# Inputs ahead of most first weights, squares on VectorE, statistics and roundings at given places

## The chip, the core and the metric

The program runs on one core of one Trainium2 chip. The metric is the device time of one execution in microseconds. TensorE (PE in the profile) multiplies, VectorE (DVE) and ScalarE (ACT) round, add and activate, GpSimd (POOL) adds and issues accumulating DMAs, SyncE (SP) issues most loads.

## What is computed

An encoder layer on two sequences of 256 tokens with 1024 features each: a feed-forward of half weight, a mixer (two recurrent branches with gates), a second feed-forward, and a last normalisation. The change touches the first feed-forward and the end of the second.

```python
def rmsnorm(x, g):
    xf = x.astype(jnp.float32)
    y = xf * lax.rsqrt(jnp.mean(xf * xf, axis=-1, keepdims=True) + EPS)
    return (y * g.astype(jnp.float32)).astype(x.dtype)

def swiglu(h, w_in, w_out):
    a, g = jnp.split(h @ w_in, [D_FF], axis=-1)
    return (jax.nn.silu(a) * g) @ w_out

def encoder_layer(x, ...):
    x = x + 0.5 * swiglu(rmsnorm(x, g_ffn1), w_ffn1_in, w_ffn1_out)
    h = rmsnorm(x, g_mix)
    ...
    x = x + merged.astype(x.dtype) @ w_out
    x = x + 0.5 * swiglu(rmsnorm(x, g_ffn2), w_ffn2_in, w_ffn2_out)
    return x

y = rmsnorm(encoder_layer(x, ...), g_final)
```

## The kernel before

**Layout.** The input stands transposed: eight tiles x0 to x7 of 128 features by 512 tokens (both sequences side by side). Every product is made of three passes, since each operand is split into a rounded high half (names with h: `xh`, `wah`, `wbh`) and a remainder, the low half (`xl`, `wal`, `wbl`). A high half is a copy on ScalarE. A low half is either a subtraction on VectorE (`split2`, L240) or, with `split_dma` (L244 to L246), a negated copy on ScalarE to which a DMA issued by POOL then adds the source once more.

**First feed-forward, first products.** `first_tiles` multiplies the eight inputs with the first six column tiles of the weights, for k = 0 to 7: three passes of six matmuls each, 18 for each k, all at L277. SP loads x_k and then the weights of k, in the order of k (L121, L123). Each weight tile is rounded when it has landed; from k = 6 on (`dma_from` 3) the low half comes by `split_dma`. `split_x` makes the two halves of x_k, scaled by the gain, and `add_sq` squares x_k on ScalarE and adds it on GpSimd to the sum `sq`.

**Statistic.** `rms_stat` runs with high priority: four small products with a column of ones sum `sq` over the features (L163, tile `ps_f1p`), ScalarE takes the root (L151, for which a table is loaded), VectorE refines the reciprocal in small steps (L152 to L156) and writes a diagonal (L177), and TensorE spreads it over all partitions (L182). ScalarE copies the result to `r` (L194). The normalisation itself is applied behind the products, in `gated`.

**Input sums and plain pairs.** `x_sums` builds, in four steps k = 0 to 3, sums and differences of quarter inputs (`xu`, `xv`, `xt`, `xw`, each scaled by `r`), which the later column tiles need; each is split (`xch`, `xcl`). Meanwhile two pairs of column tiles run as plain products (`f1p`, then `f1p2`, in `plain`, L218 to L220), each with two weight tiles of 1024 columns that `w_plain` loads and rounds by `split_dma`. Behind them `pair` runs the other column tiles (L344).

**The order.** A scheduler places instructions on each engine by priorities; `issue_after(i)` keeps what is written in it behind instruction i. At the end, in `last2`, the order of TensorE, VectorE and ScalarE is written by hand: the last residual add and its square for each half (256 tokens, one sequence), the statistic of each half, and four tiles y of each half, each sent by a DMA of its own, in turn from ScalarE's and SP's queue (L1000).

## Time and profile before

| | us |
|---|---|
| median of 3 runs | 1192.49 (1192.47 to 1193.64) |
| profiled execution | 1191.2 |
| its span | 1189.4 |
| TensorE busy | 1172.2 (99%) |
| VectorE, ScalarE, GpSimd busy | 733.0, 608.7, 115.8 |

A time in a row of the profile counts from the span's start. A row of the timeline is one instruction, or several equal ones in a row: start, duration, engine, line and operation, output and inputs with shapes, count, and in brackets how long the engine had been idle and what released it. The start of the next row can lie a little before the end of one, since instructions on an engine overlap. Buffer numbers are left out of names.

### The profile page before, as it was taken

The page shows a single profiled execution, that of the slowest core. Times are in us where ns is not written, and L with a number is a line of the kernel's source. Part 1 is how long each engine was busy: PE and PEld are TensorE (multiplying, and loading weights), DVE is VectorE, ACT ScalarE, POOL GpSimd, SP SyncE. Part 2 cuts the span into 40 slices and gives each one's busy share as a digit, 9 for nine tenths or more (in the row PEclk, how much of TensorE's full clock was granted, in tenths as well). Part 3 has the DMA queues.
Part 4 walks back from the last instruction along what each step waited for, and adds up shares of the span by engine and source line. Part 5 has one row for each costly group of instructions (what it writes and reads, how often), then busy time and mean ns, then how long its engine had stood idle before and what let it go on. Part 6 is the DMA issues. An engine that isn't in the chain of part 4 may idle for free.

```text
span 1189.4 us, 16897 instructions
## 1 busy us (share of the span) xinstructions
PE 1172.2 (99%) x6654; PEld 1016.4 (85%) x6654; DVE 733.0 (62%) x1124; ACT 608.7 (51%) x991; POOL 115.8 (10%) x143
## 2 busy tenths in 40 slices
PE   8999999999999999999999999999999999999996
PEld 6898899899987888888888888888789899989985
DVE  7974576567546888657573453363685467566643
ACT  7663365256536666575762232255664256336542
POOL 5100000000022002020000000013200000000011
PEclk9999999999999999999999999999999999999998
DMA  8763555356414213232253233141854356445512
GB/s 253 167 161 105 139 137 140 117 134 166 122 58 128 89 55 115 72 107 71 80 186 115 89 98 115 55 123 27 204 136 139 114 130 154 132 120 147 152 47 71
DMA packets 58160, 141.88 MB, mean 119 GB/s; under 512 B 5408, under 2 KB 19904, under 8 KB 58080
## 3 DMA queue, kind: packets, MB, share of 16 engines
q1 hardware_dynamic: 47664, 110.44, 29.1%
q0 software_dynamic: 8208, 27.94, 13.5%
q10 hardware_dynamic: 2208, 2.41, 0.6%
q8 instruction: 52, 0.85, 0.3%
q14 instruction: 28, 0.23, 0.1%
HBM read 135.51 MB, written 2.11 MB: 116 GB/s over the span
## 4 chain that ended last, share of the span: by engine, by line
PE 90%; issue 5%; DMA 2%; DVE 1%; POOL 1%; ACT 1%; SPq 1%; DVEq 0%; ACTq 0%; POOLq 0%
PE psy_f L344 16%; PE psq_f L344 8%; PE psz_f L344 4%; PE ps_f1o L219 3%; PE ps_f1o L220 3%; PE ps_f1o L218 3%; PE ps_f2o L219 3%; PE ps_f2o L218 3%; PE ps_f2o L220 3%; PE pt_ga L577 3%; PE pt_ga L575 3%; PE pt_ga L576 2%; PE pt_gb L577 2%; PE pt_gb L575 2%; PE pt_gb L576 2%
## 5 line engine op out<-in xcount | busy, mean ns | idle before, releaser
L344 PE MATMUL psy_f<-xch_f,wal_f2s 128*128 128x256 f32 x204 | 57.5, 282 | 0.2 <-DMA wal_f2s<-in_w_f 0.2
L344 PE MATMUL psy_f<-xch_f,wal_f1s 128*128 128x256 f32 x204 | 57.4, 281 | 0.2 <-DMA wal_f1s<-in_w_f 0.2
L344 PE MATMUL psy_f<-xch_f,wah_f2s 128*128 128x256 f32 x204 | 57.5, 282 | 0.1
L344 PE MATMUL psy_f<-xch_f,wah_f1s 128*128 128x256 f32 x204 | 57.4, 281 | 0.0
L344 PE MATMUL psy_f<-xcl_f,wah_f2s 128*128 128x256 f32 x204 | 57.4, 281 | 0.0
L344 PE MATMUL psy_f<-xcl_f,wah_f1s 128*128 128x256 f32 x204 | 57.3, 281 | 0.0
L577 PE MATMUL pt_ga<-whi_ga,xl_m 128*128 128x512 f32 x128 | 50.7, 396 | 0.0
L575 PE MATMUL pt_ga<-whi_ga,xh_m 128*128 128x512 f32 x128 | 50.6, 396 | 0.0
L577 PE MATMUL pt_gb<-whi_gb,xl_m 128*128 128x512 f32 x128 | 50.5, 396 | 0.0
L576 PE MATMUL pt_ga<-wlo_ga,xh_m 128*128 128x512 f32 x128 | 50.4, 394 | 0.0
L575 PE MATMUL pt_gb<-whi_gb,xh_m 128*128 128x512 f32 x128 | 50.4, 394 | 0.0
L576 PE MATMUL pt_gb<-wlo_gb,xh_m 128*128 128x512 f32 x128 | 50.4, 394 | 0.0
L94 DVE TENSOR_TENSOR wlo_ga<-raw_ga,whi_ga 128x1024 fp32r<-128x1024 f32 x16 | 19.6, 1225 | 46.0 <-ACT whi_ga L93 46.0
L427 DVE SCALAR_TENSOR_TENSOR x<-ps_f2o,x 128x512 f32<-128x512 f32 x23 | 15.9, 690 | 41.6 <-PE ps_f2o L220 41.6
L93 ACT CAST whi_gb<-raw_gb 128x1024 fp32r<-128x1024 f32 x16 | 16.8, 1048 | 45.7 <-PE pt_ga L577 28.8
L94 DVE TENSOR_TENSOR wlo_gb<-raw_gb,whi_gb 128x1024 fp32r<-128x1024 f32 x16 | 19.6, 1224 | 32.7 <-ACT whi_gb L93 32.5
L344 PEld LDWEIGHTS psy_f<-xch_f,wah_f2s 128*128 128x128 f32 x204 | 38.5, 189 | 0.4 <-ACT f2u L404 0.3
L344 PEld LDWEIGHTS psy_f<-xch_f,wal_f2s 128*128 128x128 f32 x204 | 38.6, 189 | 0.4 <-DMA wal_f2s<-in_w_f 0.4
L344 PEld LDWEIGHTS psy_f<-xch_f,wal_f1s 128*128 128x128 f32 x204 | 38.5, 189 | 0.5 <-DMA wal_f1s<-in_w_f 0.5
L427 DVE SCALAR_TENSOR_TENSOR x<-ps_f1o,x 128x512 f32<-128x512 f32 x24 | 16.6, 690 | 36.1 <-PE ps_f1o L220 36.1
L344 PEld LDWEIGHTS psy_f<-xch_f,wah_f1s 128*128 128x128 f32 x204 | 38.5, 189 | 0.3
L344 PEld LDWEIGHTS psy_f<-xcl_f,wah_f1s 128*128 128x128 f32 x204 | 38.4, 188 | 0.1
(1163 smaller groups left out, 4049.4 us busy)
## 6 DMA issues: line engine op xcount, KB each, us to landing
raw_f1s<-in_w_f SPq DMA_DIRECT2D x17, 512.0 KB, 3.7
wal_f1s<-in_w_f POOLq DMA_DIRECT2D x17, 512.0 KB, 5.5
raw_f2s<-in_w_f SPq DMA_DIRECT2D x17, 512.0 KB, 3.6
wal_f2s<-in_w_f POOLq DMA_DIRECT2D x17, 512.0 KB, 5.6
raw_ga<-in_w_tm SPq DMA_DIRECT2D x16, 512.0 KB, 3.6
raw_gb<-in_w_tm SPq DMA_DIRECT2D x16, 512.0 KB, 3.5
sum_f1s<-in_w_f SPq DMA_DIRECT2D x17, 256.0 KB, 3.2
raw_f1s<-in_w_f SPq DMA_DIRECT2D x17, 256.0 KB, 3.9
```

Of the source, the lines that this page charges most:

```text
L93: nc.scalar.copy(hi[:, :width], raw[:, :width])
L94: nc.vector.tensor_tensor(out=lo[:, :width], in0=raw[:, :width], in1=hi.bitcast(F32)[:, :width], op=ALU.subtract)
L218: nc.tensor.matmul(ps, lhsT=wh, rhs=xh, start=start, stop=False)
L219: nc.tensor.matmul(ps, lhsT=wh, rhs=xl, start=False, stop=False)
L220: nc.tensor.matmul(ps, lhsT=wl, rhs=xh, start=False, stop=stop)
L344: nc.tensor.matmul(ps, lhsT=l[:, f], rhs=m, start=start and k == n == 0, stop=stop and k == 3 and n == 2, skip_group_check=True)
L427: nc.vector.scalar_tensor_tensor(out=x[i], in0=ps, scalar=0.5, in1=x[i], op0=ALU.mult, op1=ALU.add)
L575: nc.tensor.matmul(pss[t], lhsT=xh, rhs=hi[:, ws], start=k == 0, stop=False)
L576: nc.tensor.matmul(pss[t], lhsT=xh, rhs=lo[:, ws], start=False, stop=False)
L577: nc.tensor.matmul(pss[t], lhsT=xl, rhs=hi[:, ws], start=False, stop=k == KD - 1)
```

## The change

The change does seven things.

1. SP's loads: x0, the weights of k = 0, x1, those of k = 1, then x2, x3, x4, the weights of k = 2, x5, x6, x7 and the weights of k = 3 to 7.
2. The first activation of the program, a dummy, is Sqrt instead of a copy; the table that it loads is the one that the statistic needs.
3. In the first feed-forward the squares are no longer made in `split_x`: at k = 0 that of x0, at k = 1 those of x1 to x4, at k = 2 those of x5 to x7 (`squares`), and they are added by VectorE instead of GpSimd.
4. `rms_stat` takes two places (`places`): the sums stand behind the last matmul of pass 1 at k = 2, the broadcast behind that of pass 2 at k = 3.
5. `dma_from` is 4, so the low halves of k = 6 and 7 are subtractions on VectorE.
6. The roundings of the plain pairs stand behind steps of the input sums (`rounds`): the second tile of the first pair and the first tile of the second pair behind step k = 1, the second tile of the second pair behind step k = 2. The first tile of the first pair has no such bound.
7. In `last2` the diagonal of half 0 is written ahead of the residual add of half 1, its broadcast stands ahead of the sums of half 1, and two of the four y of half 0 come ahead of the reciprocal of half 1.

```diff
+    def load_first(k): ...
+    def load_x(k):
+        nc.sync.dma_start(x[k], xT[k * P:(k + 1) * P, :])
+    for k in range(2):
+        load_x(k)
+        load_first(k)
         if k == 0:
             nc.scalar.dma_start(pt, par)
+    for k in range(2, 5):
+        load_x(k)
+    load_first(2)
+    for k in range(5, KD):
+        load_x(k)
+    for k in range(3, KD):
+        load_first(k)
-    nc.scalar.activation(act0, ones[:, 0:1], AF.Copy, scale=2.0)
+    nc.scalar.activation(act0, ones[:, 0:1], AF.Sqrt)
...
+    def at(i):
+        return tc.issue_after(i) if i is not None else ExitStack()
...
-    def rms_stat(sq, name, banks=(None, None)):
+    def rms_stat(sq, name, banks=(None, None), behind=(None, None)):
         with tc.high_priority():
-            rc = rms_cols([sq], range(4), name, banks[0])
-            ps = spread(rc, name, banks[1])
+            with at(behind[0]):
+                st = rms_sum([sq], range(4), name, banks[0])
+            rc = small(f"rc_{name}", 4)
+            rsqrt(rc, st, 1.0 / D, name)
+            dg = diag(rc, name)
+            with at(behind[1]):
+                ps = broadcast(dg, name, banks[1])
...
-            nc.gpsimd.tensor_tensor(out=sq, in0=sq, in1=t, op=ALU.add)
+            (nc.vector if name == "a" else nc.gpsimd).tensor_tensor(out=sq, in0=sq, in1=t, op=ALU.add)
...
                 xs.append(xs_of(k))
+                for n in squares.get(k, ()):
+                    add_sq(n, sq, "a")
...
+                    marks[k, n] = nc.tensor.matmul(pss[m], lhsT=w[:, f[m]], rhs=xp, start=k == n == 0,
+                                                   stop=k == KD - 1 and n == 2).ins
...
                 x_last[:] = [split2(*hl, src).ins]
+                marks["x", k] = rounded[0]
...
-            split_dma(hi, lo, raw, w_a[2 * j + n])
+            with at(behind[n - first]):
+                split_dma(hi, lo, raw, w_a[2 * j + n])
...
-        w_p = w_plain(w_a, NP, f"{name}p")
+        w_p = w_plain(w_a, NP, f"{name}p", (None, None) if rounds is None else (None,))
         for _ in range(4):
             next(steps)
+        if rounds is not None:
+            w_p += w_plain(w_a, NP, f"{name}p", (marks["x", rounds[0]],), 1)
         gated(top, pss[2 * top], pss[2 * top + 1])
-        w_p2 = w_plain(w_a, NP + 1, f"{name}p2")
+        w_p2 = w_plain(w_a, NP + 1, f"{name}p2", (None, None) if rounds is None else [marks["x", n] for n in rounds])
...
-    ffn(w_f1, w_o1, lambda k: split_x(k, C_G1, sq1, "a"), raw1, 3, C_G1, sq1, "f1", done1)
+    ffn(w_f1, w_o1, lambda k: split_x(k, C_G1, None, "a"), raw1, 4, C_G1, sq1, "f1", done1,
+        squares={0: (0,), 1: range(1, 5), 2: range(5, KD)}, places=((2, 1), (3, 2)), rounds=(1, 2))
...
+            dg = [diag(rc[0], "f0")]
             final(1)
-            dg = [diag(rc[0], "f0")]
+            rf = [broadcast(dg[0], "f0")]
             st.append(rms_sum([sq_of("f"), sql], (2, 3), "f1"))
-            rf = [broadcast(dg[0], "f0")]
+            scaled(0, rf[0], range(0, 2))
             rsqrt(rc[1], st[1], 1.0 / D, "f1")
             dg.append(diag(rc[1], "f1"))
             rf.append(broadcast(dg[1], "f1"))
-            for half in range(2):
-                scaled(half, rf[half])
+            scaled(0, rf[0], range(2, KD // 2))
+            scaled(1, rf[1], range(KD // 2))
```

TensorE in the first products, before: the digit after `xh_a`, `xl_a` is k, `wah_f1i1` and `wal_f1i1` are the halves of the weights of k = 2 and 3, `dg_f1` is the diagonal. This is the place of the broadcast.

```order
L277 MATMUL ps_f1i4_147<-xh_a3_238,wal_f1i1_208 128x512
L277 MATMUL ps_f1i5_148<-xh_a3_238,wal_f1i1_208 128x512
L182 MATMUL ps_f1p1_378<-dg_f1_392,ones_75 128x512
L277 MATMUL ps_f1i0_143<-xl_a3_239,wah_f1i1_207 128x512
L277 MATMUL ps_f1i1_144<-xl_a3_239,wah_f1i1_207 128x512
```

The same place of TensorE now:

```order
L295 MATMUL ps_f1i4_147<-xl_a3_254,wah_f1i1_216 128x512
L295 MATMUL ps_f1i5_148<-xl_a3_254,wah_f1i1_216 128x512
L192 MATMUL ps_f1p1_376<-dg_f1_390,ones_75 128x512
L295 MATMUL ps_f1i0_143<-xh_a4_279,wah_f1i2_275 128x512
L295 MATMUL ps_f1i1_144<-xh_a4_279,wah_f1i2_275 128x512
```

The broadcast moved from ahead of the last pass of k = 3 to behind it; the four sums (L163) moved from the middle of the first pass of k = 3 to behind the second pass of k = 2.

ScalarE among the input sums, before: `xch_f1` with two digits is the high half of a sum of the step that the first of the two digits names, `f1p1` is the second tile of the first plain pair, `f1p20` the first of the second.

```order
L239 CAST xch_f10_424<-xu_f10_414 128x256
L244 CAST wbh_f1p20_497<-sum_f1p20_495 128x1024
L239 CAST xch_f100_428<-xv_f10_415 128x512
L239 CAST xch_f10_424<-xu_f11_440 128x256
L245 ACTIVATE wbl_f1p20_498<-sum_f1p20_495 128x1024
L239 CAST xch_f101_432<-xt_f10_416 128x512
L239 CAST xch_f102_436<-xw_f10_417 128x512
L239 CAST xch_f110_452<-xv_f11_441 128x512
L245 ACTIVATE wal_f1p1_410<-raw_f1p1_407 128x1024
L239 CAST xch_f111_456<-xt_f11_442 128x512
L244 CAST wah_f1p1_409<-raw_f1p1_407 128x1024
L239 CAST xch_f112_460<-xw_f11_443 128x512
```

The same place of ScalarE now:

```order
L254 CAST xch_f10_415<-xu_f10_405 128x256
L254 CAST xch_f100_419<-xv_f10_406 128x512
L254 CAST xch_f101_423<-xt_f10_407 128x512
L254 CAST xch_f102_427<-xw_f10_408 128x512
L254 CAST xch_f10_415<-xu_f11_431 128x256
L254 CAST xch_f110_443<-xv_f11_432 128x512
L254 CAST xch_f111_447<-xt_f11_433 128x512
L254 CAST xch_f112_451<-xw_f11_434 128x512
L259 CAST wah_f1p1_483<-raw_f1p1_481 128x1024
L254 CAST xch_f12_465<-xu_f12_455 128x256
L260 ACTIVATE wal_f1p1_484<-raw_f1p1_481 128x1024
L259 CAST wbh_f1p20_495<-sum_f1p20_493 128x1024
```

The four roundings that stood among the copies of steps k = 0 and 1 now stand behind the last copy of step k = 1.

VectorE at the end, before: `x7` is the last residual add (of half 1), `dg_f0` the diagonal of half 0, `y` with two digits is the tile and the half.

```order
L156 SCALAR_TENSOR_TENSOR rc_f0_10843<-s_f0_10846,rc_f0_10843 128x2
L985 SCALAR_TENSOR_TENSOR x7_85<-ps_f2l1_10791,x7_85 128x256
L987 TENSOR_TENSOR sql_10789<-x7_85 128x256
L177 TENSOR_SCALAR dg_f0_10855<-pt_77,rc_f0_10843 128x128 x2
L152 TENSOR_SCALAR v_f1_10865<-st_f1_10858 128x2
L153 RECIPROCAL rc_f1_10844<-s_f1_10866 128x2
```

VectorE at the end now:

```order
L169 SCALAR_TENSOR_TENSOR rc_f0_10841<-s_f0_10844,rc_f0_10841 128x2
L187 TENSOR_SCALAR dg_f0_10851<-pt_77,rc_f0_10841 128x128 x2
L1010 SCALAR_TENSOR_TENSOR x7_85<-ps_f2l1_10789,x7_85 128x256
L1012 TENSOR_TENSOR sql_10787<-x7_85 128x256
L1020 TENSOR_TENSOR y00_10863<-xg00_10573,sp_f0_10856 128x512
L1020 TENSOR_TENSOR y10_10866<-xg01_10643,sp_f0_10856 128x512
L165 TENSOR_SCALAR v_f1_10869<-st_f1_10858 128x2
L166 RECIPROCAL rc_f1_10842<-s_f1_10870 128x2
```

The diagonal of half 0 moved ahead of the residual add, and two y of half 0 moved ahead of the steps of half 1. On ScalarE the DMA of the first y now stands between the roots of the two halves; both roots stood ahead of all output DMAs before.

## Rows read from the trace of the kernel before

**Rows 1.** The page, busy us (share of the span) and instructions of the engines.

```profile
PE 1172.2 (99%) x6654; PEld 1016.4 (85%) x6654; DVE 733.0 (62%) x1124; ACT 608.7 (51%) x991; POOL 115.8 (10%) x143
```

**Rows 2.** Waits of TensorE, whole span: us in total, times, longest.

```profile
PE ps_f1p L163 <- POOL sq L215: 1.6, 1, 1.6
PE ps_f1p L182 <- DVE dg_f L177: 1.4, 1, 1.4
```

**Rows 3.** Chain that ended last, 0 to 30 us: start, us, what.

```profile
10.29 1.45 SPq L121
...
12.26 6.80 DMA x<-in_xT
```

**Rows 4.** Timeline of TensorE, first feed-forward.

```profile
6.65 1.64 PE L277 MATMUL ps_f1i<-xh_a,wbh_f1i 128*128 128x512 f32 x6 [0.75 <-DVE xh_a L201]
...
17.92 1.57 PE L277 MATMUL ps_f1i<-xl_a,wah_f1i 128*128 128x512 f32 x6
...
21.78 1.05 PE L163 MATMUL ps_f1p<-ones,sq 128*128 128x1 f32 x8 [1.60 <-POOL sq L215]
...
45.54 0.39 PE L218 MATMUL ps_f1p<-xh_a,wbh_f1p 128*128 128x512 f32 x1
```

**Rows 5.** Busy time of a stretch: us, engines, granted clock, DMA share, GB/s.

```profile
12.00:14.00 2.00, 2.00 (x11) 1.59 (x10) 2.00 (x3) 1.94 (x4) 1.70 (x1) 1.00 1.12 323
```

**Rows 6.** Timeline of ScalarE, first products and statistic.

```profile
8.15 0.84 ACT L239 CAST wbh_f1i<-raw_first 128x768 fp32r<-128x768 f32 x1 [0.39 <-DMA raw_first<-in_w_f]
8.89 0.72 ACT L203 ACTIVATE xh_a<-x,pt 128x512 fp32r<-128x512 f32 x1
...
22.91 1.28 ACT L151 ACT_TABLE_LOAD   x1 [2.59 <-PE ps_f1p L163]
```

**Rows 7.** Timeline of VectorE, first products and input sums.

```profile
6.89 0.74 DVE L204 SCALAR_TENSOR_TENSOR xl_a<-x,pt,xh_a 128x512 fp32r<-128x512 f32 x1
7.55 0.55 DVE L240 TENSOR_TENSOR wbl_f1i<-raw_first,wbh_f1i 128x384 fp32r<-128x384 f32 x1
8.02 1.79 DVE L204 SCALAR_TENSOR_TENSOR xl_a<-x,pt,xh_a 128x512 fp32r<-128x512 f32 x1
9.73 0.95 DVE L240 TENSOR_TENSOR wbl_f1i<-raw_first,wbh_f1i 128x768 fp32r<-128x768 f32 x1
...
34.25 0.70 DVE L240 TENSOR_TENSOR xcl_f<-xt_f,xch_f 128x512 fp32r<-128x512 f32 x1
```

**Rows 8.** Timeline of ScalarE, last copy of the sums' step k = 1.

```profile
38.36 0.62 ACT L239 CAST xch_f<-xw_f 128x512 fp32r<-128x512 f32 x1
```

**Rows 9.** DMA issues, 0 to 40 us: count, KB each, median us to landing.

```profile
wal_f1i<-sum_first POOLq DMA_DIRECT2D x2, 384.0 KB, 9.4
wal_f1p<-in_w_f POOLq DMA_DIRECT2D x1, 512.0 KB, 6.7
```

**Rows 10.** Timeline of VectorE at the end.

```profile
1176.13 0.16 DVE L156 SCALAR_TENSOR_TENSOR rc_f<-s_f,rc_f 128x2 f32<-128x2 f32 x1
...
1178.45 0.16 DVE L152 TENSOR_SCALAR v_f<-st_f 128x2 f32<-128x2 f32 x1 [0.82 <-ACT s_f L151]
...
1179.37 0.48 DVE L177 TENSOR_SCALAR dg_f<-pt,rc_f 128x128 f32<-128x128 f32 x2
1179.77 1.88 DVE L995 TENSOR_TENSOR y<-xg,sp_f 128x512 f32<-128x512 f32 x3
...
1184.41 0.48 DVE L998 SCALAR_TENSOR_TENSOR y<-x,pt,sp_f 128x256 f32<-128x256 f32 x1
```

**Rows 11.** Timeline of TensorE at the end, the two broadcasts.

```profile
1177.97 0.83 PE L182 MATMUL sp_f<-dg_f,ones 128*128 128x256 f32 x2
1179.91 1.22 PE L182 MATMUL sp_f<-dg_f,ones 128*128 128x256 f32 x2 [1.11 <-DVE dg_f L177]
```

**Rows 12.** Output DMAs: one issue of ScalarE's queue; landings of the tensor.

```profile
1180.48 0.40 ACTq L1000 DMA_DIRECT2D out_yT<-y  x1
...
DMA to landing us min/median/max: 2.2/2.8/3.4
```

More of the change, by code (lines that the diff above doesn't have):

```diff
@@ L119, in encoder_kernel, with load_first @@
             for kp in range(4)]
-    for k in range(KD):
-        nc.sync.dma_start(x[k], xT[k * P:(k + 1) * P, :])
+    def load_first(k):
         for n in ((range(0, 3), range(3, NF)) if k == 0 else (range(NF),)):
@@ L165, in rms_sum @@
         return ps
-    def rms_cols(parts, cs, name, bank=None):
-        r = small(f"rc_{name}", len(cs))
-        rsqrt(r, rms_sum(parts, cs, name, bank), 1.0 / D, name)
-        return r
     def diag(r, name):
@@ L183, in broadcast @@
         return ps
-    def spread(r, name, bank=None):
-        return broadcast(diag(r, name), name, bank)
-    def rms_stat(sq, name, banks=(None, None)):
+    def rms_stat(sq, name, banks=(None, None), behind=(None, None)):
         with tc.high_priority():
-            rc = rms_cols([sq], range(4), name, banks[0])
-            ps = spread(rc, name, banks[1])
+            with at(behind[0]):
[5 more added lines that the diff above has]
+                ps = broadcast(dg, name, banks[1])
             r = rp.tile([P, T], F32, tag="r", name=f"r_{name}")
@@ L205, in split_x @@
                                        op0=ALU.mult, op1=ALU.subtract)
-        add_sq(k, sq, name)
+        if sq is not None:
+            add_sq(k, sq, name)
         return hi, lo
@@ L236, in gemm @@
         return ps
+    rounded = []
     def split2(hi, lo, src):
-        nc.scalar.copy(hi, src)
+        rounded[:] = [nc.scalar.copy(hi, src).ins]
         return nc.vector.tensor_tensor(out=lo, in0=src, in1=hi.bitcast(F32), op=ALU.subtract)
@@ L246, in split_dma, with first_tiles @@
         nc.gpsimd.dma_start(lo, again, accum_op=ALU.add)
-    def first_tiles(raws, xs_of, dma_from, name):
+    def first_tiles(raws, xs_of, dma_from, name, sq, squares):
         pss = [acc(f"ps_{name}{m}", m >= 4) for m in range(NF)]
         xs = []
+        marks = {}
         for kp in range(4):
@@ L276, in first_tiles, with x_sums @@
                     w, xp = passes[n]
-                    nc.tensor.matmul(pss[m], lhsT=w[:, f[m]], rhs=xp, start=k == n == 0,
-                                     stop=k == KD - 1 and n == 2)
-        return pss, xs
+                    marks[k, n] = nc.tensor.matmul(pss[m], lhsT=w[:, f[m]], rhs=xp, start=k == n == 0,
+                                                   stop=k == KD - 1 and n == 2).ins
+        return pss, xs, marks
     x_last = []
-    def x_sums(gcol, r, name):
+    def x_sums(gcol, r, name, marks):
         res = [[] for _ in range(7)]
@@ L352, in activate, with w_plain @@
         return h
-    def w_plain(w_a, j, name):
+    def w_plain(w_a, j, name, behind, first=0):
         res = []
-        for n, (get, pool, w) in enumerate(((w_sum, "wb", 2), (w_raw, "wa", 5))):
+        tiles = ((w_sum, "wb", 2), (w_raw, "wa", 5))
+        for n in range(first, first + len(behind)):
+            get, pool, w = tiles[n]
             raw = get(f"{name}{n}")[:, 0:2].rearrange("p a b -> p (a b)")
@@ L372, in w_out_tile, with ffn @@
         return hi, lo
-    def ffn(w_a, w_o, xs_of, raws, dma_from, gcol, sq, name, done, last=None):
+    def ffn(w_a, w_o, xs_of, raws, dma_from, gcol, sq, name, done, last=None, squares={}, places=(None, None), rounds=None):
         L, R = slice(0, SEQ), slice(SEQ, T)
@@ L442, in ffn @@
                               lambda w, part=part, i=i: out_tile(part, i, w)))
-        pss, xs = first_tiles(raws, xs_of, dma_from, f"{name}i")
+        pss, xs, marks = first_tiles(raws, xs_of, dma_from, f"{name}i", sq, squares)
         banks = [[acc(f"ps_{name}p{n}", True) for n in range(2)]]
-        r, _ = rms_stat(sq, name, banks[0])
+        r, _ = rms_stat(sq, name, banks[0], [marks.get(m) for m in places])
         act_of = {}
@@ L467, in ffn @@
         top = NP - 1
-        steps = x_sums(gcol, r, name)
-        w_p = w_plain(w_a, NP, f"{name}p")
+        steps = x_sums(gcol, r, name, marks)
+        w_p = w_plain(w_a, NP, f"{name}p", (None, None) if rounds is None else (None,))
         for _ in range(4):
             next(steps)
+        if rounds is not None:
+            w_p += w_plain(w_a, NP, f"{name}p", (marks["x", rounds[0]],), 1)
         gated(top, pss[2 * top], pss[2 * top + 1])
-        w_p2 = w_plain(w_a, NP + 1, f"{name}p2")
+        w_p2 = w_plain(w_a, NP + 1, f"{name}p2", (None, None) if rounds is None else [marks["x", n] for n in rounds])
         xc += next(steps)
@@ L987, in final, with scaled @@
             nc.vector.tensor_tensor(out=sql[:, cs], in0=x[i][:, cs], in1=x[i][:, cs], op=ALU.mult)
-        def scaled(half, rf):
+        def scaled(half, rf, ns):
             cs, rf = cut[half], rf.unsqueeze(1)
-            for n_ in range(KD // 2):
+            for n_ in ns:
                 y = tmp(f"y{n_}{half}", (P, 2, SEQ))
```

## Prediction

> **What bounds the kernel now.** I read the page's busy shares first, then TensorE's waits over the whole run, then its timeline for the start, then the end. TensorE is busy for 1172.2 of 1189.4 us [rows 1]: a stage is worth what it makes TensorE wait. The two longest waits in the table stand in the first feed-forward: 1.6 us at the statistic's sums (L163), released by GpSimd's last add, and 1.4 us at the broadcast of the statistic (L182), released by VectorE [rows 2]. They are the first place where this change can gain. The second is after the last product, where VectorE writes the outputs. All that lies between is bound by TensorE's own matmuls, so what is gained at the start should be carried to the end.
>
> Why do the two waits stand there? The sums of squares need all eight inputs, and x7, the last, lands at 12.26 + 6.80 = 19.06 [rows 3], because each input is loaded just ahead of its weights. Then follow its square, a GpSimd add and the statistic at 21.78. The matmuls of the first weights come in groups of six at 1.40 us: from 6.65 the ninth group starts at 17.92 [rows 4]. With 24 groups (33.6 us), the statistic (1.05) and a broadcast of about that length, the stage from 6.65 to the first plain product at 45.54 [rows 4] would take 35.7 us and takes 38.89: the excess is 3.2, which agrees with the waits of 1.6 and 1.4.
>
> **The change part by part. Loads.** The same bytes leave in another order. The queue moves 323 GB/s [rows 5], and the weights of k = 1 land at 8.15, when their rounding starts [rows 6]. Ahead of x7 there are from then on six inputs (0.262 MB each) and one k of weights (0.393 MB): 1.97 MB, 6.1 us, so x7 lands at 14.2 and not at 19.06. The weights pay: k = 2 lands at 11.8, k = 3 at 15.5, k = 4 at 16.7, k = 5 at 17.9, k = 7 still at 20.3. TensorE wants them at 6.65 + 4.2 k, that is at 15.1, 19.3 (20.2 with the statistic ahead), 25 and 29. Rounding costs 0.84 on ScalarE and 0.95 on VectorE [rows 6, 7]. Each k has over 2 us to spare: nothing on the path. SP's plain loads stay behind these; the first one waits for the low half of k = 3 (about 18.3 for 16.96) and its product starts after 42. Nothing either.
>
> **Squares on VectorE.** Seven adds of the form 128x512 cost 0.70 each, 0.62 with the overlap of 0.08 that the starts 6.89 and 7.55 show [rows 7]: 4.3 us more for VectorE. Against that, the adds on GpSimd leave this stretch: beside them the low half of an input took 1.79 and, before the first of them, 0.74 [rows 7]. Some six such instructions lose a microsecond each, so VectorE comes out with less to do. When is the last add done? ScalarE is in order: from 8.15 one rounding (0.74 to the next), then sq2, xh2, sq3, sq4, xh3 (0.63 each, the 0.72 of a scaled copy less an overlap of 0.1 [rows 6]), the rounding of k = 2, xh4, sq5, sq6, sq7 end at 15.3 and xh5 at 15.9. VectorE, with xl3 at 12.1, then add, low half of k = 2, add, xl4, add, xl5, add, at 0.66, 0.62 and 0.87 each, ends at 17.4. The new place of the sums is behind the eighth group, at 17.92. So 0.5 us are left, and the 1.6 us wait goes. This is the closest margin of the forecast.
>
> **The Sqrt table and the broadcast.** The table load of 1.28 stands between the statistic and its root [rows 6]; it moves to the start, in place of the load that is there anyway. The sums end at about 18.9, the root at 19.2. VectorE then finishes the low half of k = 5 (20.0), has two input halves (xl6, xl7, 1.4) between the small steps and about 1.9 for the rest: ready at 23.3. The new place of the broadcast, behind all of k = 3, is 17.92 + 1.0 + 5.6 = 24.5. With 1.2 to spare the 1.4 us wait goes too. **Term one: 3.1 us** (bounds 3.05, the two waits, and 3.4, with the matmuls' overlap lost at each stop); below, if an add is late, one for one.
>
> **Weights k = 6, 7.** Two accumulating DMAs on POOL and two negated copies on ScalarE go; VectorE gets two subtractions of 0.95, ahead of the input sums. These weights are wanted at 33 and 38; their buffer comes free when TensorE ends k = 3, at 24.5. They are rounded by 28. Nothing on the path, but the input sums start at 27 to 28 and gain little over the time before.
>
> **Roundings behind steps.** The second half of the first plain pair is rounded behind the sums' step k = 1, ended by a copy that started at 38.36 before [rows 8]. Now no plain rounding stands ahead of that copy among the sums: 35 to 38.4. With the copy (0.62), the cast, one copy and the negated copy, 3.1 in all, the accumulating DMA is issued at 38.1 to 41.5 and lands 6.7 later [rows 9]: 44.8 to 48.2. TensorE wants it after the first half (24 matmuls, 5.6): first plain product 42.4, so 48.0, and the low half two matmuls later. Nothing in most of that span; with 9.4, the longest landing in the same answer [rows 9], a wait of up to 2.4. The second pair has 11 us more. I take nothing, since 6.7 is this very transfer.
>
> **The end.** The diagonal of half 0 now goes ahead of the last residual add: the root's last step ends at 1176.29, so the diagonal (0.48) runs to 1176.88 and the broadcast (0.83) to 1177.8 [rows 10, 11]; the residual add and the square are pushed back by 0.4. y0 and y1 of half 0 fill VectorE from 1177.8 to 1179.0, where it idled 0.82 [rows 10]. The price is on ScalarE: the issue of y0's output DMA (0.40 [rows 12]) stands ahead of half 1's root. y0 ends at 1178.5, the issue at 1178.93, the root at 1179.2; the rest of the chain takes 1.3 (1178.45 to 1179.77): y2 at 1180.5. Its halves end at 1181.9, as does the second broadcast (1.22 [rows 11]); half 1 takes 2.6, half of the 5.12 from 1179.77 to 1184.89 [rows 10], and the last y is done at 1184.5 for 1184.89. Gain 0.4. In addition the eight outputs left some 0.6 apart, faster than they drained: landings run from 2.2 to 3.4 [rows 12], 0.17 more for each. With two sent 2 us ahead of the other six I expect some two steps of backlog at the last, 2.6. **Term two: 0.4 + 0.8 = 1.2**, bounds 0.3 and 1.6.
>
> [...]
>
> **Sum.** 3.1 + 1.2 = 4.3 us. The profiled execution took 1191.2 (span 1189.4 and 1.8 around it): 1186.9. The median of the runs shown is 1192.49, 1.3 above it, and I forecast against that: 1188.2. A measurement of this kernel can tell about 0.2% from no change, 2.4 us: below 1190.1 is faster, above 1194.9 slower.
>
> **Rivals.** *The squares come late.* ScalarE's twelve steps or the loads slip. For it: only 0.5 us of margin, and the adds are chained. Against it: every term is a row of the same stretch. If x7 landed as late as before, the add would end at about 20.4, 2.5 behind its place: 1190.7, inside 0.2%. A slip of one microsecond gives 1188.7. Chance 0.13.
>
> *The root of half 1 is held by the output's issue.* If an issue takes 1.45, as one of SP's input issues did [rows 3], and not 0.40, half 1 is 1.05 later, and with less backlog at the end term two falls to about 0.3: 1189.1. Against it: at the start the queue was full, at the end it is empty. Chance 0.12.
>
> *Slower: the second half of the first plain pair.* Place: its low half, behind the input sums, the copies and POOL. Price: one for one beyond 48.5. To eat 4.3 it must land at 52.8; to be slower by 0.2%, at 55.2, thus with a landing of 9.4 be issued after 45.8, from a step k = 1 that ends over 4 us later than before. Against it: that step's work has lost the roundings ahead of it. Result 1195 or more. Chance 0.04; and 0.04 for a wait of some 2 us there, 1190.3.
>
> The Trainium skill names a way to such a late landing: by "SBUF — State Buffer", section "SBUF: two separate sides", VectorE in its two-port mode keeps GpSimd from writing descriptors. No run before isolates it; the 6.7 was measured while VectorE had hardly any idle time.
>
> *The change doesn't do what it says*: the place of the statistic is fixed by the order, so this could only be the end's order having no effect: 1189.4. Chance 0.05.
>
> **How the numbers follow.** Forecast 0.62 (own range 1187.0 to 1189.3), squares 0.13, held root 0.12, plain wait 0.04, slower 0.04, no effect at the end 0.05. The range takes the forecast's bounds (sums of 5.0 and 3.35, and half a microsecond for the spread of the runs shown) and reaches to 1190.6 on the side of the rivals: 1187.0 to 1190.6. Faster: forecast, held root, end, and 0.07 of the squares, the smaller slips: 0.86. Within 0.2%: the rest of the squares and the plain wait: 0.10. Slower: 0.04.
>
> **What would show it.** Right: no wait of TensorE at the sums and the broadcast; x7 at about 14 us; the first plain product at 42.4; at the end, which lies 3.1 earlier as a whole, the first y begun at about 1174.7 instead of 1179.77 and the last one done at 1181.4 instead of 1184.89. Wrong: a wait behind the eighth group released by VectorE's add, a wait at a plain product released by a DMA from POOL, or ScalarE's second root over a microsecond behind y0.

## The result and the profile after

The changed kernel takes 1186.7 us, the median of 4 executions (1186.2 to 1187.17), where the kernel before takes 1192.8 in the same comparison (1192.47 to 1193.64): a ratio of 0.9948, with a 95% interval of 0.9931 to 0.9965. It is faster by 6.1 us; the interval is a gain of 4.2 to 8.2, since the executions of before spread. The prediction had the sign and the places right, but said 1188.2, with a lower bound of 1187.0: the gain is 1.8 us larger than the 4.3 it forecast, and the time lies just below the range.

The profiled execution of the changed kernel took 1186.62, with a span of 1184.8. Against the profiled execution of before (1191.2) that is 4.58 us, close to the 4.3. So most of the miss does not lie between the two traces that were compared; it lies between before's trace and before's other executions. That is what the experiments are about.

First the page's busy line, and two entries of TensorE's waits (us in total, times, longest), the first of the list and the longest wait for a DMA:

```profile
PE 1171.9 (99%) x6654; PEld 1017.6 (86%) x6654; DVE 731.0 (62%) x1133; ACT 605.9 (51%) x988; POOL 102.8 (9%) x134
```

```profile
PE sp_f L192 <- DVE dg_f L187: 2.7, 2, 2.1
...
PE psy_f L363 <- DMA wal_f1s<-in_w_f: 0.3, 1, 0.3
```

TensorE is as busy as before [rows 1] in a span that is 4.6 us shorter; GpSimd has lost 13 us. The two longest waits of before, at the sums and at the broadcast of the first statistic [rows 2], are gone from the list. What heads it now stands behind the last product, where TensorE has nothing else to do; no wait for a DMA is longer than 0.3.

The timeline of TensorE in the first feed-forward (start, length, instructions; an idle stretch would stand in brackets at the row's end), then those of VectorE and of ScalarE around the statistic:

```profile
18.10 0.95 PE L179 MATMUL ps_f1p<-ones,sq 128*128 128x1 f32 x8
...
24.55 1.02 PE L192 MATMUL ps_f1p<-dg_f,ones 128*128 128x512 f32 x2
...
42.14 0.39 PE L231 MATMUL ps_f1p<-xh_a,wbh_f1p 128*128 128x512 f32 x1
```

```profile
16.88 0.68 DVE L228 TENSOR_TENSOR sq<-sq,sq_a 128x512 f32<-128x512 f32 x1
...
22.00 0.88 DVE L187 TENSOR_SCALAR dg_f<-pt,rc_f 128x128 f32<-128x128 f32 x4
```

```profile
19.14 0.26 ACT L164 ACTIVATE s_f<-ps_f1p,eps 128x4 f32<-128x4 f32 x1 [0.51 <-PE ps_f1p L179]
```

The last square is added by 17.56, half a microsecond ahead of the sums; the root follows them with no table load in between; the diagonal is done at 22.88, 1.7 ahead of the broadcast. The first plain product starts at 42.14, where it started at 45.54 [rows 4]: 3.40.

VectorE at the end, and the landings of the output (shortest, median, longest):

```profile
1172.58 0.48 DVE L187 TENSOR_SCALAR dg_f<-pt,rc_f 128x128 f32<-128x128 f32 x2
...
1173.92 1.29 DVE L1020 TENSOR_TENSOR y<-xg,sp_f 128x512 f32<-128x512 f32 x2
1175.39 0.16 DVE L165 TENSOR_SCALAR v_f<-st_f 128x2 f32<-128x2 f32 x1 [0.18 <-ACT s_f L164]
...
1176.32 0.48 DVE L187 TENSOR_SCALAR dg_f<-pt,rc_f 128x128 f32<-128x128 f32 x2
...
1180.16 0.47 DVE L1023 SCALAR_TENSOR_TENSOR y<-x,pt,sp_f 128x256 f32<-128x256 f32 x1
```

```profile
DMA to landing us min/median/max: 2.2/2.4/3.1
```

Two outputs now fill the place where VectorE idled 0.82 [rows 10], and the longest landing is 3.1 where it was 3.4 [rows 12].

To compare executions I cut each trace at the same three instructions: the first plain product, the first matmul of the last statistic (half 0), and the end of the last output product. The middle column is the whole work between the first two. All times are us of the profiled execution.

| kernel | its time | first plain product | middle | last statistic to last product | from there to the end |
|---|---|---|---|---|---|
| before | 1191.20 | 45.54 | 1128.65 | 10.70 | 4.51 |
| before, again (e1) | 1193.41 | 47.64 | 1128.29 | 10.70 | 4.97 |
| changed | 1186.62 | 42.14 | 1128.23 | 10.26 | 4.17 |
| changed, again (e2) | 1186.25 | 41.51 | 1128.47 | 10.34 | 4.18 |
| new start, old end (e3) | 1187.47 | 42.11 | 1128.21 | 10.82 | 4.56 |
| old start, new end (e4) | 1192.24 | 47.22 | 1128.79 | 10.26 | 4.23 |

The middle differs by up to 0.6 with no clear order between the kernels. The start differs by 2.1 between two executions of the very same kernel before.

### The profile page after: what moved, and what is told of

The parts are those of the page before. It is cut to its first block, busy times and chain, and to the rows that moved or that the text cites. A ratio compares the mean times of both kernels' runs of the same rounds, so it can differ in the third digit from the quotient of the medians.

```text
span 1184.8 us, 16884 instructions
## 1 busy us (share of the span) xinstructions
PE 1171.9 (99%) x6654; PEld 1017.6 (86%) x6654; DVE 731.0 (62%) x1133; ACT 605.9 (51%) x988; POOL 102.8 (9%) x134
## 4 chain that ended last, share of the span: by engine, by line
PE 90%; issue 5%; DVE 2%; ACT 1%; DMA 1%; POOL 1%; DVEq 0%; ACTq 0%; POOLq 0%
PE psy_f L363 16%; PE psq_f L363 8%; PE psz_f L363 4%; PE ps_f1o L232 3%; PE ps_f1o L231 3%; PE ps_f1o L233 3%; PE ps_f2o L232 3%; PE ps_f2o L231 3%; PE ps_f2o L233 3%; PE pt_ga L602 3%; PE pt_ga L600 3%; PE pt_ga L601 3%; PE pt_gb L602 2%; PE pt_gb L600 2%; PE pt_gb L601 2%
```

## The experiments

**Both kernels again, and the change cut in two.** The first question was where the 1.5 us beyond the traces' 4.6 come from: from nowhere but the draw of the executions (theory A), or from a start of before that is longer in most executions than in the one profiled (theory B). e1 is the kernel before and e2 the changed one, both unedited. e3 is the changed kernel with the end's order of before:

```diff
-            dg = [diag(rc[0], "f0")]
             final(1)
-            rf = [broadcast(dg[0], "f0")]
+            dg = [diag(rc[0], "f0")]
             st.append(rms_sum([sq_of("f"), sql], (2, 3), "f1"))
-            scaled(0, rf[0], range(0, 2))
+            rf = [broadcast(dg[0], "f0")]
...
-            scaled(0, rf[0], range(2, KD // 2))
-            scaled(1, rf[1], range(KD // 2))
+            for half in range(2):
+                scaled(half, rf[half])
```

and e4 the kernel before with the same lines the other way round.

> The kernel before, once more, unchanged. Theory A (the gain lies in the traces, and the profiled execution of before was a fast one, 1.3 us under the median of the other runs): the ratio to before is 1.000, the runs spread over 1191.2 to 1193.6, and this trace has the same two waits, 1.6 at the sums and 1.4 at the broadcast. Theory B (the start of before is unsteady: x7 or the last add comes later in most executions than in the profiled one): the ratio is 1.000, but the two waits together come out at 4 us or more in this trace, with the first plain product at 46.5 or later.

> The changed kernel, once more, unchanged. Theory A: on one chip with before it gains what the two traces show, 4.6 us (ratio 0.996), and its own runs spread as wide as those of before. Theory B: it gains 6 us (ratio 0.995), and its runs spread less than those of before, since its places of the statistic have room that absorbs a late input.

> The change with the end undone (last2 as before). Theory A: it gains 3.4 at the start and perhaps 0.4 along the way, 1189 against 1192.8 (ratio 0.997), and its end takes as long as that of before. Theory B: 5.2 us (ratio 0.9956).

> The kernel before with the new end alone (last2 as changed). Both theories: 0.8 us faster by the two traces (last y 0.44 earlier, the longest landing 3.1 for 3.4), ratio 0.9993; the prediction's second term was 1.2 (0.999). A third theory, that the end gives more in the median than in the traces, has 2 us or more (0.998).

Measured, beside 21 executions of before on the same chip (1192.81, from 1191.37 to 1194.39): e1 1192.25 (1191.51 to 1194.01), e2 1186.59 (1186.25 to 1186.78), ratio 0.9950 with 0.9937 to 0.9964; e3 1187.69 (1187.41 to 1188.58), 0.9961 with 0.9949 to 0.9974; e4 1191.03 (1190.5 to 1193.3), 0.9987 with 0.9978 to 0.9996. Of the difference the start alone gives 5.1 us and the end alone 1.8, or 1.1 by the step from e3 to e2. The 1.8 is more than the 0.8 expected of e4; part of it is that only 2 of e4's 11 executions have the low mean clock that is described next.

Kernels with the old start spread over 2.5 to 3 us, those with the new start over 0.5 to 1.2. That was theory B's sign, but its reason fell. B said that in before's longer executions x7 and the last addition come later. This is TensorE's timeline in e1:

```profile
21.88 1.05 PE L163 MATMUL ps_f1p<-ones,sq 128*128 128x1 f32 x8 [1.40 <-POOL sq L215]
...
23.59 2.40 PE L277 MATMUL ps_f1i<-xh_a,wal_f1i 128*128 128x512 f32 x6
26.57 2.04 PE L182 MATMUL ps_f1p<-dg_f,ones 128*128 128x512 f32 x2 [0.59 <-DVE dg_f L177]
27.63 3.45 PE L277 MATMUL ps_f1i<-xl_a,wah_f1i 128*128 128x512 f32 x6
...
47.64 0.39 PE L218 MATMUL ps_f1p<-xh_a,wbh_f1p 128*128 128x512 f32 x1
```

The sums start at 21.88 instead of 21.78 [rows 4]: nothing is late there, and the waits are shorter (1.40 and 0.59 for 1.60 and 1.45). What is longer are the matmuls behind the waits: six take 2.40 and 3.45. The view of busy time by stretches tells why. Its columns are the stretch, its length, the busy time of the five engines, the granted clock of TensorE, the DMA share and GB/s; first e1, then the execution of before that the prediction was made from, then one row of e4:

```profile
24.00:26.00 2.00, 1.98 (x5) 1.01 (x4) 1.76 (x9) 1.99 (x4) 0.00 (x0) 0.50 0.77 250
26.00:28.00 2.00, 1.43 (x3) 0.84 (x3) 0.43 (x3) 1.19 (x2) 1.22 (x2) 0.50 0.44 66
28.00:30.00 2.00, 2.00 (x5) 1.30 (x4) 0.64 (x1) 1.33 (x2) 0.72 (x1) 0.50 0.76 242
```

```profile
24.00:26.00 2.00, 1.02 (x5) 0.50 (x3) 1.75 (x9) 1.99 (x4) 0.00 (x0) 1.00 0.79 254
26.00:28.00 2.00, 1.53 (x5) 1.00 (x6) 0.33 (x2) 1.49 (x3) 1.32 (x2) 1.00 0.40 72
```

```profile
24.00:25.00 1.00, 1.00 (x4) 0.81 (x3) 0.62 (x1) 0.99 (x3) 0.00 (x0) 0.50 0.54 119
```

In e1 the granted clock is 0.50, the lower of its two levels, 1.2 GHz, from 24.0 to 30.8 us (read in stretches of half a microsecond). In the execution that the prediction read it is 1.00 from 8 to 50 us. The same fall stands in e4's trace, from 22.3 to 29.2 us behind a wait of 1.70. In e1 it comes behind the first wait and before the second, which ends at 26.57. Over all 70 executions of before that were timed beside these experiments, 19 have a mean granted clock of 0.992 or 0.993 over the whole run and all of those take 1193.07 us or more; the other 51 have 0.994 or more and a median of 1192.16, and four of them are longer than 1193.07 too. This gave **theory C**: a wait can cost more than its length, because behind it TensorE's clock falls in some executions; without waits it should not.

**The waits filled.** If C holds, matmuls that nobody reads, put into the two waits, must keep the clock up without making either statistic earlier. They change nothing of what is computed.

```diff
...
-    def rms_stat(sq, name, banks=(None, None)):
+    def rms_stat(sq, name, banks=(None, None), fills=(None, None)):
         with tc.high_priority():
+            if fills[0] is not None:
+                fill(banks[0], fills[0], 6)
             rc = rms_cols([sq], range(4), name, banks[0])
+            if fills[1] is not None:
+                fill(banks[1], fills[1], 5)
             ps = spread(rc, name, banks[1])
...
```

> The kernel before, with matmuls that nothing reads put into its two waits in the first tiles: six of 128x512 right ahead of the sums of squares (in the trace of before that place stood idle for 1.60 us, six take about 1.4), five right ahead of the broadcast (idle for 1.45 us in one execution, 0.59 in another, five take about 1.2). Neither statistic can come earlier by that. Theory C (the clock): in the execution of before that has the longer span the granted clock reads 0.50 from 24 to 30 us, right behind the two waits, and 1.00 in the shorter one; the waits make the clock fall in some executions, and that is the 1.3 us which the prediction carried over. Then the clock stays at 1.00 here, the first plain product starts at 45.3 to 46.0, the median is 1191.2 to 1192.0 and the spread goes below 1.2. Theory W (the waits themselves are of changing length, or the excess lies elsewhere): median 1192.6 to 1193.2, spread about 3 as before.

Measured: 1192.36 (1190.96 to 1193.89) beside before's 1192.54. No execution has a mean clock below 0.995, but neither theory's time came out: the planner, with other work around the statistic, had put a rounding of 1.05 us ahead of the root on ScalarE, so the diagonal came late, TensorE waited 1.0 us at the broadcast, and the first plain product started at 46.33:

```profile
22.68 1.05 ACT L256 CAST wbh_f1p<-sum_f1p 128x1024 fp32r<-128x1024 f32 x1 [2.55 <-DMA sum_f1p<-in_w_f]
```

```profile
27.22 1.12 PE L190 MATMUL ps_f1p<-dg_f,ones 128*128 128x512 f32 x2 [1.01 <-DVE dg_f L185]
```

Inconclusive for the time. Its spread of 2.9, without a fall of the clock, is what theory W expected: not all of the spread is the clock. So the run was made again with that rounding held behind the root:

```diff
...
-            split_dma(hi, lo, raw, w_a[2 * j + n])
+            with at(root[0] if name == "f1p" and n == 0 else None):
+                split_dma(hi, lo, raw, w_a[2 * j + n])
...
```

> The kernel before with the two waits filled as in the last such run, and the rounding of the first plain weights held behind the statistic's root: in that run the planner had moved this rounding (1.05 us) ahead of the root, so the first plain product started at 46.33 instead of 45.54 and the time had a cause of its own to be longer. Theory C: with the root back in its place and no idle stretch of over half a microsecond but the rest of the second wait, the clock stays at 1.00, no execution has a mean granted clock under 0.995, and the median is 1191.2 to 1191.9 with a spread below 1.5. If the waits' clock is not what makes before's executions differ: median 1192.5 to 1193 with the same two heaps as before.

Measured: 1191.79 (1191.27 to 1192.47, 11 executions) beside 1192.31 (1191.86 to 1194.0); ratio 0.9994, interval 0.9985 to 1.0003. Median and spread are those that theory C expected. TensorE's timeline of it:

```profile
20.17 1.55 PE L166 MATMUL ps_f1p<-xh_a 128*128 128x512 f32 x6
21.78 1.05 PE L173 MATMUL ps_f1p<-ones,sq 128*128 128x1 f32 x8
...
24.86 1.31 PE L166 MATMUL ps_f1p<-xh_a 128*128 128x512 f32 x5
26.38 1.13 PE L192 MATMUL ps_f1p<-dg_f,ones 128*128 128x512 f32 x2 [0.22 <-DVE dg_f L187]
...
45.48 0.39 PE L232 MATMUL ps_f1p<-xh_a,wbh_f1p 128*128 128x512 f32 x1
```

The sums stand at 21.78 and the first plain product at 45.48, as in the prediction's execution [rows 4]: the fills took the place of the waits and gained nothing else. The spread is 1.2 us, and over e5 and e9 none of 22 executions has a mean clock below 0.995; of the 70 of before 40 have, and 19 are below 0.994. The clock's fall is thus tied to the waits. The shift of the median, 0.5 us, lies within its interval: a change of the median is not shown by this run, and it says nothing of what the fall costs the executions that meet it.

**The squares on GpSimd again.** The changed kernel with one line of it undone; TensorE's order is the same.

```diff
-            (nc.vector if name == "a" else nc.gpsimd).tensor_tensor(out=sq, in0=sq, in1=t, op=ALU.add)
+            nc.gpsimd.tensor_tensor(out=sq, in0=sq, in1=t, op=ALU.add)
```

> The changed kernel with the seven additions of the first squares given back to GpSimd; PE's order is the same. GpSimd took 1.6 to 1.7 us for one, beside 0.74 us on VectorE; seven of them behind x1's square end at about 20.5, so the sums, whose place comes at 18.1, wait about 2.4 us, and the root behind them comes at 25.3 instead of 22.9, where the broadcast's place has moved to 27: no second wait. Waits alone: 1186.6 + 2.4 = 1189.0, with the spread of 0.5 that the changed kernel has. Theory C: in part of the executions the clock falls behind the wait too, so the median is 1189 to 1192 and the spread 2 or more, with the granted clock at 0.50 for about 6 us in the slower ones.

Measured: 1190.76 (1188.48 to 1192.9, 12 executions), 0.9983 of before with 0.9973 to 0.9992. Five executions lie at 1188.48 to 1189.29, with a mean clock of 0.996 or 0.997: that fits the wait alone, expected at 1189.0, though none of the five is the profiled one. The four longest, 1191.14 to 1192.9, have 0.993 or 0.994. Three lie between, at 1190.46 to 1191.11 with 0.996, and are not explained. The profiled execution is the longest of them. Its wait, and its granted clock behind the wait:

```profile
PE ps_f1p L179 <- POOL sq L228: 2.6, 1, 2.6
```

```profile
22.00:24.00 2.00, 2.00 (x6) 1.61 (x7) 2.00 (x3) 0.27 (x1) 0.00 (x0) 0.50 0.76 215
24.00:26.00 2.00, 2.00 (x7) 1.52 (x6) 1.79 (x10) 0.95 (x1) 0.00 (x0) 0.50 0.92 332
26.00:28.00 2.00, 2.00 (x7) 1.57 (x6) 0.13 (x1) 1.05 (x2) 0.62 (x1) 0.56 0.60 240
```

So a single late step in an otherwise unchanged kernel brings the fall back in a part of the executions. And the addition's engine is the largest of the parts of the start that are undone here one by one: 4.2 us of the median, 2.3 in the five executions that fit the wait alone.

The timelines of GpSimd and of VectorE in the same execution show how the additions hold VectorE up:

```profile
13.56 6.95 POOL L228 TENSOR_TENSOR sq<-sq,sq_a 128x512 f32<-128x512 f32 x4
```

```profile
15.93 3.47 DVE L216 SCALAR_TENSOR_TENSOR xl_a<-x,pt,xh_a 128x512 fp32r<-128x512 f32 x2
...
21.26 0.74 DVE L216 SCALAR_TENSOR_TENSOR xl_a<-x,pt,xh_a 128x512 fp32r<-128x512 f32 x1
```

One addition takes GpSimd 1.74 us (the shortest in the trace of before takes 1.26), and VectorE's low half of an input takes 1.74 beside it and 0.74 once GpSimd is through, at 20.51. The Trainium skill, page "SBUF — State Buffer", section "SBUF: two separate sides", says that the port pair which VectorE and GpSimd share is held by one whole instruction at a time; these rows agree.

**The loads interleaved again.** The changed kernel with each x ahead of its own weights, as before.

```diff
-    for k in range(2):
+    for k in range(KD):
         load_x(k)
         load_first(k)
...
-    for k in range(2, 5):
-        load_x(k)
-    load_first(2)
-    for k in range(5, KD):
-        load_x(k)
-    for k in range(3, KD):
-        load_first(k)
```

> The changed kernel with x and the first weights loaded in turns again, all else as changed. x7 then lands at about 19 instead of 14.2; its square and addition end at 20.6, and the sums wait 2.5 us at their place of 18.1. So the loads carry most of the gain at the start if the median goes to 1189.1 (the wait's length alone) or higher (with the clock's fall, up to 1192, spread 2 or more); if GpSimd's slow additions had been the whole cause, the median stays within 0.7 of 1186.6.

Measured: 1187.8 (1187.61 to 1187.99), 0.9961 of before with 0.9949 to 0.9973: 1.2 us behind the changed kernel, where I had put 2.5. TensorE's timeline and VectorE's:

```profile
20.94 1.05 PE L172 MATMUL ps_f1p<-ones,sq 128*128 128x1 f32 x8 [0.58 <-DVE sq L221]
```

```profile
20.20 0.69 DVE L221 TENSOR_TENSOR sq<-sq,sq_a 128x512 f32<-128x512 f32 x1
```

The last addition ends at 20.89, close to the 20.6 expected, but the planner moved the sums back by eight matmuls, since a given place is only the earliest one. So the wait is 0.58 and the first plain product starts at 43.24, 1.1 later than in the changed kernel. The spread stays at 0.4: no fall of the clock behind this wait. So the loads, undone alone and with the sums moved, carry 1.2 us, less than the additions' engine.

**The statistic placed by the planner.** The changed kernel without the given places.

```diff
-        squares={0: (0,), 1: range(1, 5), 2: range(5, KD)}, places=((2, 1), (3, 2)), rounds=(1, 2))
+        squares={0: (0,), 1: range(1, 5), 2: range(5, KD)}, rounds=(1, 2))
```

> The changed kernel with the statistic placed by the planner again. It puts the sums seven matmuls (1.6 us) earlier, at about 16.5, while the last addition ends at 17.6: a wait of about 1.1 us; the broadcast stands eight matmuls earlier, at about 23.7 with that wait, and the diagonal comes at 23 to 24, a wait of 0 to 0.5. Waits alone: 1186.6 + 1.1 to 1.6 = 1187.7 to 1188.2, spread 0.5. Theory C with waits this short: the clock may stay up (the same) or fall in part of the executions (1188 to 1190.5, spread 2 or more); which of the two tells how long a wait it takes here.

Measured: 1188.05 (1187.69 to 1189.96), 0.9967 with 0.9955 to 0.9979. The rows of TensorE:

```profile
17.35 1.05 PE L179 MATMUL ps_f1p<-ones,sq 128*128 128x1 f32 x8 [0.98 <-DVE sq L228]
...
23.68 1.02 PE L192 MATMUL ps_f1p<-dg_f,ones 128*128 128x512 f32 x2
```

One wait of 0.98 and a first plain product at 43.13: the places carry 1.0 us of the start's 3.4. With 1.1 for the loads and 2.3 for the additions' engine that makes 4.4, more than the start as a whole: the parts overlap, so none of these can be read as a share of the gain. Four of the five executions lie within 1.0 us of each other, one at 1189.96 has a mean clock of 0.995 and may have met the fall; the profiled one did not.

**The table's move and the roundings' places.** First the square root's table loaded behind the sums again:

```diff
-    nc.scalar.activation(act0, ones[:, 0:1], AF.Sqrt)
+    nc.scalar.activation(act0, ones[:, 0:1], AF.Copy, scale=2.0)
```

> The changed kernel with its first activation a copy again, so the square root's table is loaded (1.28 us) between the sums and the root. In the changed kernel the diagonal ends at 22.9 and the broadcast's place comes at 24.55, 1.7 later: the load should fit, with 0.3 us to spare. My theory: 1186.6, no wait at the broadcast, the load hidden. If the root's later end also pushes VectorE's small steps behind the low halves that it does between them, a wait of up to 0.7: 1187.3.

Measured: 1186.57 (1186.2 to 1187.05), no difference. ScalarE's load, and VectorE's diagonal behind it:

```profile
19.16 1.28 ACT L164 ACT_TABLE_LOAD   x1
20.45 0.27 ACT L164 ACTIVATE s_f<-ps_f1p,eps 128x4 f32<-128x4 f32 x1
```

```profile
22.68 0.88 DVE L187 TENSOR_SCALAR dg_f<-pt,rc_f 128x128 f32<-128x128 f32 x4
```

The root ends 1.3 later than in the changed kernel (20.72 for 19.40), the diagonal only 0.7 later (23.56 for 22.88, with the broadcast at 24.41), since VectorE had other steps to do in between. Then the plain pairs' roundings without their given steps (`rounds` left out of the call):

> The changed kernel with the plain pairs' roundings not held behind steps of the input sums: the planner may put them ahead of the copies among the sums again. The prediction priced this part at nothing. So 1186.6 with an interval over no change, the first plain product at 42.1, and no wait of TensorE in the plain products; if holding them back carries a part of the gain, 1187 to 1188 and a wait in the plain products or the first use of the input sums.

Measured: 1186.58 (1186.31 to 1187.15), no difference, with the first plain product at 41.96. The planner does place roundings among the sums' copies there, and TensorE waits for none of them. ScalarE's row of one, which in the changed kernel stands behind step k = 1:

```profile
32.97 1.06 ACT L260 ACTIVATE wal_f1p<-raw_f1p 128x1024 fp32r<-128x1024 f32 x1
```

Neither part of the change is worth anything measurable here. For the roundings that is as priced; the table's move the prediction had counted among the reasons for the broadcast's wait to go.

**The first output on SyncE.** The one rival that showed in the trace is the root of half 1 behind the first output's issue. It can be taken away:

```diff
-                (nc.sync if n_ % 2 else nc.scalar).dma_start(out3[n_, :, :, cs], y)
+                (nc.sync if n_ % 2 or n_ == half == 0 else nc.scalar).dma_start(out3[n_, :, :, cs], y)
```

> The changed kernel with the first output transfer issued by SyncE instead of ScalarE. In the changed kernel this issue (0.40 us) stands on ScalarE ahead of half 1's root, which starts at 1175.10 where the sums' last matmul ends at about 1174.75; VectorE then waits 0.18 us for it. Without it the root starts 0.3 earlier and VectorE's wait of 0.18 goes: 1186.4, within the spread; the trace is to show the last output product 9.1 us behind half 0's root, where it is 9.28 now. If SyncE's six issues in place of five hold the last output: 1186.6 or a little more.

Measured: 1186.48 (1185.86 to 1186.92): by time the same as the changed kernel. VectorE's rows behind the first two outputs:

```profile
1174.49 1.29 DVE L1020 TENSOR_TENSOR y<-xg,sp_f 128x512 f32<-128x512 f32 x2
1175.69 0.15 DVE L165 TENSOR_SCALAR v_f<-st_f 128x2 f32<-128x2 f32 x1
...
1180.45 0.48 DVE L1023 SCALAR_TENSOR_TENSOR y<-x,pt,sp_f 128x256 f32<-128x256 f32 x1
```

The wait of 0.18 is gone, the last output product ends 9.01 us behind half 0's root, where 9.1 was expected, and from the last statistic to the last product it takes 9.99 instead of 10.26 to 10.35 in all the other kernels with the new end. The middle of this execution was the longest of all (1129.07), which hides it in the profiled time. It is the best version here by its end; by its median it cannot be told from the changed kernel.

## Why the prediction was off, step by step

- **Loads and squares.** Right. The last addition was put at 17.4 and ended at 17.56; the sums' place at 17.92 and came at 18.10; the margin of 0.5 held. ScalarE's squares of x5 to x7 ended at 14.82 (15.3 in the prediction) without a wait between them, so x7 had landed by about 14, as forecast. The margin is as thin as said: in e10's execution the sums waited 0.2 for that addition.
- **Table and broadcast.** The diagonal was put at 23.3 and was done at 22.88; the broadcast at 24.5 and came at 24.55. The table load's move, counted among the reasons, turned out to be worth nothing by itself (e10).
- **Term one, 3.1 us**, bounds 3.05 to 3.4: measured 3.40, at the upper bound. The reason named for that bound, the overlap of matmuls that each stop costs, fits; no run isolates it.
- **Weights k = 6, 7, and roundings behind steps, nothing.** Right: no wait of TensorE for them; the low half of the first pair's second tile was issued at 38.43, in the forecast span (38.1 to 41.5), and e11 shows the free order of the roundings to cost the same. No run undoes `dma_from` by itself.
- **Term two, 0.4 + 0.8.** The chain was right: from the last statistic to the last product it is 10.26 for 10.70, a gain of 0.44. The landing was mis-sized: from the last product to the end it took 4.17 for 4.51, a gain of 0.34 and not 0.8. The longest landing went to 3.1, not to 2.6. The first y began at 1173.92 for 1174.7 and the last was done at 1180.63 for 1181.4; those 0.8 are the start's 0.3 and the middle's 0.4 that the forecast did not have, and 0.05 of the chain.
- **Sum, 4.3.** Between the two profiled executions it is 4.58 (4.6 by their spans): 3.40 + 0.44 + 0.34, and 0.42 from the middle, which differs that much from one execution to another. That the sum came so close is in part luck: the middle's 0.42 makes up for what the landing fell short by, 0.46.
- **"The median of the runs shown is 1192.49, 1.3 above it, and I forecast against that."** This is the step that failed. It carried an excess of before over to the changed kernel, as if it were a constant, and gave no cause for it; without it the forecast was 1186.9, 0.2 from the measured 1186.7. It was not a constant: before's median of 1192.8 is 1.6 above its profiled execution, the changed kernel's 1186.7 only 0.1 above its own. That difference of 1.5 is most of the 1.8 that the gain was missed by; the other 0.3 is the sum's (4.58 for 4.3). What before's excess is made of is shown in part. 1191.2 is shorter than all but 2 of the 70 executions of before that were timed later. That execution kept its clock up behind both waits, as 19 of the 70, by their mean clock, did not; but the other 51 have a median of 1192.16, still 1.0 above it, so the clock is the smaller part. It also had the shortest end of the five traces with the old end (4.51, where the others have 4.56 to 5.10, and a longest landing of 3.4 or 3.9). The changed kernel has no wait at the start behind which the clock could fall: none of its nine executions has a mean clock below 0.996. And in all nine traces with the new end it takes 4.11 to 4.23.
- **The forecast's own range.** Its upper end of 1189.3 does not follow from its terms: 1192.49 less 3.35 is 1189.1, with half a microsecond 1189.6. Nothing hangs on it.

How much of the 6.1 us each of these is can only be bounded. With the clock kept up by the fills, before takes 1191.79 (e9), so the fall is worth at most some 0.5 of the median (0.25 by the 70 executions, 1192.41 with and 1192.16 without the 19), and 1.7 to 2.1 us in the executions that it meets (the 19 against the 51 by their medians, 1193.88 against 1192.16; and 47.64 against 45.54 by the traces). From 1191.79 to 1186.6 there are 5.2: 3.3 to 3.4 at the start, 0.44 in the last chain, and 0.4 to 0.9 in the landings. The last two make 0.8 to 1.3, which agrees with the end's 1.1 from e3 to e2 and with e4, whose nine executions with a mean clock of 0.995 or more have a median of 1191.0, 1.2 below that of the 51. So in the medians the second term, 1.2, came out about as forecast, though 0.78 between the two profiled executions. Some 0.4 to 1.1 us is left that no run here assigns, and its cause stays open. The middle is 0.2 longer on average in the five traces with the old start (1128.71 for 1128.47), which is within its scatter.

Of the rivals, late squares did not come, nor the wait in the first plain pair. The held root did, in small: the issue took 0.41, not 1.45, and cost VectorE 0.18 us of waiting, some 0.3 in all (e12). The end's order does have an effect (e3 to e2: 1.1 us).

## What to carry to other kernels

A profiled execution is one draw: before its time is subtracted from, look where it lies among the other executions, and ask whether what makes them differ is something that the change removes. A wait of TensorE early in a kernel can cost twice, once by its length and again by the clock behind it, so its price is a range from the length up to the length and half the stretch at the lower clock (the numbers stand in the next section). Where a place for an instruction is given as the earliest one, a planner can still move it back, and an experiment that relies on the place has to read the order anew.

## What the runs showed of the hardware

- TensorE's granted clock fell to 0.50 for 6.8 us behind waits of 1.40 (e1), 1.70 (e4) and 2.6 us (e6), and did not behind waits of 1.60 and 1.45 in another execution of the same kernel as e1, nor in the profiled executions behind 0.98 (e8) or 0.58 (e7). The same program with the same waits meets it in some executions and not in others.
- The fall comes when TensorE is at work again: 0.4 us after the sums have begun in e4 and e6, 2.1 us after it in e1 (22 to 24 us still read 1.00). The stretch at 0.50 ends while TensorE works on.
- What it costs: the first plain product stands 5.50 (e1), 5.08 (e4) and 5.73 us (e6) behind that of the changed kernel, and the waits are 1.99, 1.70 and 2.60 of it. The rest, 3.1 to 3.5, is about half of the 6.8. With the old start the fall costs less on balance, 2.1 (e1) and 1.7 (e4) against the 45.54 of before, because the second wait shrinks with it: 0.59 and none, for 1.45.
- At the end of the program the clock falls as well: before's first trace reads 0.50, e2 0.52 and the changed kernel's first trace 0.76 in the stretch from 10 to 5 us before the end. There it costs little: the chain to the last product takes 10.34 in e2 and 10.26 in the changed kernel's first trace.
- An addition of 128x512 takes 1.74 us on GpSimd beside VectorE's low halves, and 0.68 on VectorE; while GpSimd adds, VectorE's low half of an input takes 1.74 for 0.74. Moving the seven additions to VectorE made both engines' work shorter: from e6 to the changed kernel VectorE's busy time goes from 734.2 to 731.0 us and GpSimd's from 114.9 to 102.8.
